# A second copy of the input, tokens along the partitions, for the first norm's sums of squares

## The chip, the cores and the metric

The kernel runs on one core of a Trainium2 chip, as one launch. The metric is the time of one execution on the device in microseconds (us). TensorE is called PE in the profile, VectorE DVE, ScalarE ACT, GpSimd POOL; SP is the engine whose queue issues the transfers here.

## The reference, cut to what matters

Two layers work on 256 tokens of 2048 features, in fp32. Layer 0 mixes by a long convolution beside a pool, layer 1 by a short convolution; each is followed by a gated feed-forward part (5632 wide), and a last norm ends it. Each part begins with an RMS norm; the first is that of the input x:

```python
def rms_norm(x, g):
    xf = x.astype(jnp.float32)
    y = xf * lax.rsqrt(jnp.mean(xf * xf, axis=-1, keepdims=True) + EPS)
    return (y * g.astype(jnp.float32)).astype(x.dtype)

def conv_pool_mixer(x, norm_g, w_in, conv_w, conv_b, ln_g, ln_b, w_pool, pool_scale, w_out):
    h = rms_norm(x, norm_g)
    u = h @ w_in
    a_val = u[..., :D_CONV]
    a_gate = u[..., D_CONV:2 * D_CONV]
    b_in = u[..., 2 * D_CONV:]
    a = a_val * jax.nn.sigmoid(a_gate)
    a = causal_depthwise_conv(a, conv_w) + conv_b
    a = jax.nn.silu(layer_norm(a, ln_g, ln_b))
    p = multiscale_pool(b_in, w_pool, pool_scale)
    return jnp.concatenate([a, p], axis=-1) @ w_out
```

## The kernel before, in words

Activations lie with features along the partitions: `h` holds 16 chunks of 128 features by 256 tokens. A product takes, for each chunk of outputs, one 128x128 block of weights for each of the 16 input chunks. Products must be as exact as fp32, so each weight and each activation is split into two fp32r halves, `hi` and `lo`, and a block costs three matmuls of 256 columns: hi times hi (L155), hi times lo (L156), lo times hi (L157). Later parts use a wide form with two matmuls (L152, L153).

The weights are one stream in the order of their use. `fetch` (L95 to L99) loads a unit of it on SP's queue, first 1, 3 and 4 blocks, then seven units of 8 blocks, then units of 16 blocks (1 MB). Four buffers hold the units, so a unit waits until the one four before it has been split. `prepare` (L101 to L111) makes the halves of a piece of 8 blocks: ACT casts it to `hi` (L109), DVE subtracts to get `lo` (L110). `next_block` (L113) does this four pieces ahead of the block that PE takes next. The framework orders each engine's instructions by a timeline of its own, with the written order as the priority: an instruction that is written later can be issued earlier, if what stands ahead of it still waits. Once built, each engine takes its instructions in that fixed order.

The start: x is loaded transposed, one or two chunks at a time (`load`, L320), between the first units of weights. For each chunk ACT and DVE multiply by the norm's gain and split into `xs` (`split`, L188 and L189). The factor 1/rms of each token is not needed for that: it is applied to the products' outputs. It comes from sums of squares: for each pair of chunks `square2` (L277) has ACT square 128x512 numbers (L280) and POOL add them to a running tile (L282). `rstd` (L287) calls `rsqrt_of` (L217): PE sums the running tile over the partitions by matmuls with a column of ones (L223), which leaves one number per token, tokens along the partitions, in two columns; ACT takes the square root (L225); DVE forms the reciprocal and corrects it (L226 to L231) and makes diagonal matrices of the factors (`diag`, L235); PE spreads them to all partitions (L243); DVE copies the result to `rstd` (L290).

The first product makes four chunks of outputs together (L411), so that each step over one input chunk takes four blocks; `loads_behind` (L327) issues the last loads of x and the rest of the vectors `v` behind the first steps. Then DVE scales the four outputs by `rstd` (L310), and the convolution begins: 31 taps a chunk, shared between POOL (with ACT's products, L364 and L366) and DVE (L375, L377), beside the further products of the mixer.

Of the kernel before, what the change touches and what calls it, by code (L numbers as in the profile page):

```python
# [11 lines left out]
F32 = mybir.dt.float32  # L12
F32R = mybir.dt.float32r
AF = mybir.ActivationFunctionType
ALU = mybir.AluOpType
PSUM = bass.MemoryType.PSUM

P = 128
T = 256
D = 2048  # L20
# [8 lines left out]
EPS = 1e-6  # L29
WINDOWS = (2, 4, 8, 16)  # L30

# the order of the first product's output after its first four chunks: chunks of the convolution,
# and groups of the pool
M0_ORDER = (
# [5 lines left out]

# columns of the per-feature vectors, one column per chunk of 128 features
VECS = {}
# [9 lines left out]

# blocks of 128x128 weights in the order of their use
N_BLOCKS = 24 * NC + 16 + NC * NC + 2 * (2 * NF * NC + NC * NF) + 48 * NC + NC * NC
# [10 lines left out]
UNIT_AT = [sum(UNITS[:u]) for u in range(len(UNITS))]  # L65
# units are split into halves in pieces: (unit, first block, blocks)
PIECE = 8
PIECES = [(u, o, min(PIECE, n - o)) for u, n in enumerate(UNITS) for o in range(0, n, PIECE)]
# pieces that are split, and units that are loaded, before they are needed
LOOK = 4  # L70
AHEAD = 1
# products that the tensor engine turns over before the first operands are there
WARM = 9
# taps of each pair of chunks of the long convolution that GpSimd adds up (VectorE takes the rest),
# and the pace of the work beside the matrix products in blocks a step
CONV = {1: (0, 2, 20), 3: (2, 2, 20), 5: (4, 2, 19), 6: (6, 1, 18), 7: (7, 1, 18)}
# [3 lines left out]
@with_exitstack  # L80
def block_kernel(ctx: ExitStack, tc: tile.TileContext, xT: bass.AP, vec: bass.AP, wall: bass.AP, out: bass.AP):
    nc = tc.nc
# [7 lines left out]

# [1 line left out]
    loaded, ready = {}, {}  # L92
    cursor = [0, 0]  # next block, piece of the next block

# [33 lines left out]

# [1 line left out]
    queues = {name: deque() for name in ("pool", "dve", "ln", "wait")}  # L130
# [28 lines left out]
    def matmul_chunks(xs, ks, n=1, wide=False, behind=None):  # L159
        """n chunks of 128 output features: hi*hi + hi*lo + lo*hi. When wide, columns 0:T hold  # L160
        hi*hi and T:2T the cross terms."""
        accs = [ps.tile([P, 2 * T], F32, name="acc") for _ in range(n)]
        for i, k in enumerate(ks):
            first, last = i == 0, i == len(ks) - 1
            for acc in accs:
                hi, lo = next_block()
                product(acc, hi, lo, xs[:, k, :], first, last, wide)
                tick()
            if behind is not None:
                behind(k)  # L170
        return accs

    phase = [None]  # the pool of the part of the kernel that is being built

# [7 lines left out]
    def split(dst, src, scale=None):  # L182
        """dst[:, :T], dst[:, T:] = fp32r halves of src (times a scale per feature)."""
        if scale is None:
            nc.scalar.copy(dst[:, :T], src)
            nc.vector.tensor_tensor(out=dst[:, T:], in0=src, in1=dst[:, :T], op=ALU.subtract)
        else:
            nc.scalar.activation(dst[:, :T], src, AF.Copy, scale=scale)  # L188
            nc.vector.scalar_tensor_tensor(out=dst[:, T:], in0=src, scalar=scale, in1=dst[:, :T], op0=ALU.mult, op1=ALU.subtract)  # L189

# [1 line left out]
    v = const.tile([P, NVEC], F32, name="v")  # L192
# [8 lines left out]
    nc.gpsimd.memset(ones, 1.0)  # L201
    # the tensor engine's clock rises after some microseconds of work
    idle = ps_st.tile([P, P], F32, name="idle", tag="st")
# [12 lines left out]

    def rsqrt_of(*totals, scale, halves=False):  # L217
        """(scale * sum over features and over totals + EPS) ** -0.5 per token, in every partition,
        if asked for in two halves. Tokens lie along the partitions in between."""
        st = ps_st.tile([P, 2], F32, name="st", tag="st")  # L220
        for i, x in enumerate(totals):
# [18 lines left out]
    def over_features(x):  # L240
        """Sum over the partitions, in every partition."""
        st = ps_st.tile([P, T], F32, name="st", tag="st")
        nc.tensor.matmul(st, ones, x, start=True, stop=True)  # L243
        return st

    class Norm:
        """RMS norm: h * gain goes into xs chunk by chunk; the factor per token follows."""

# [27 lines left out]

        def square2(self, c):  # L277
            """A pair of chunks."""
            into = tmp.tile([P, 2, T], F32, name="sum2" if c == 0 else "sq2", tag="sum2" if c == 0 else "gate", bufs=1 if c == 0 else 2)
            nc.scalar.activation(into, h[:, c : c + 2, :], AF.Square)  # L280
            if c:
                nc.gpsimd.tensor_tensor(out=self.pairs, in0=self.pairs, in1=into, op=ALU.add)  # L282
            else:
                self.pairs = into
                self.sums = [into[:, 0, :], into[:, 1, :]]

        def rstd(self):  # L287
            st = rsqrt_of(*self.sums, scale=1.0 / D)
            r = tmp.tile([P, T], F32, name="rstd", bufs=1)
            nc.vector.tensor_copy(out=r, in_=st)  # L290
            return r

    def project(src, ks, norm=None, wide=False, narrow_end=False):
        """h += src @ weights, and the next norm behind it."""
        for n in range(NC):
            if narrow_end and n == NC - 1:
                wide = False
            (acc,) = matmul_chunks(src, ks, wide=wide)
            if wide:
                t = phase[0].tile([P, T], F32, name="cross", bufs=3)  # L300
                nc.scalar.copy(t, acc[:, T:])
                nc.vector.tensor_tensor(out=h[:, n, :], in0=h[:, n, :], in1=t, op=ALU.add)
            nc.vector.tensor_tensor(out=h[:, n, :], in0=acc[:, :T], in1=h[:, n, :], op=ALU.add)
            if norm is not None:
                norm.add(n)
# [9 lines left out]

# [1 line left out]
    norm = Norm("mix_norm_e")  # L317
    nc.sync.dma_start(v[:, :NC], vec[:, :NC])

    def load(at, n):  # L320
        nc.sync.dma_start(h[:, at : at + n, :], xT[:, at : at + n, :])
        for c in range(at, at + n):
            norm.scale(c)
        if (at + n) % 2 == 0:
            norm.square2(at + n - 2)

    def loads_behind(k):  # L327
        if k < 3:
            load(10 + 2 * k, 2)
        if k == 2:  # L330
            nc.sync.dma_start(v[:, NC:], vec[:, NC:])

    load(0, 1)
    prepare(0)
# [11 lines left out]
    with tc.tile_pool(name="m0", bufs=1) as m0:  # L346
# [9 lines left out]
        def tap(c, n, k):  # L356
            """GpSimd's taps of n chunks."""
            dst = conv[:, c : c + n, :] if k == 0 else m0.tile([P, 2, T], F32, name="prod", bufs=4)[:, :n, :]
# [9 lines left out]
        def side_tap(c, n, k, first):  # L368
            """VectorE's taps, in a sum of their own."""
            if k == first:  # L370
# [18 lines left out]
        def convolve(c, n, taps):  # L389
            """The causal convolution of n chunks."""  # L390
            left = [2]
# [19 lines left out]
        first = matmul_chunks(xs, every, n=4, behind=loads_behind)  # L411
        r = norm.rstd()
        nc.scalar.activation(warm, r[:, :1], AF.Sigmoid)
# [4 lines left out]
        def pooled(g):  # L418
            """Windowed means minus the value, for a group of the pool."""
            w = WINDOWS[g]  # L420
# [29 lines left out]

        # layer norm over the features of the convolution, beside the pool's output projection
        state = {}
# [66 lines left out]

# [1 line left out]
    after = Norm("mix_norm_o")  # L521
    swiglu(norm, after)

# [1 line left out]
    norm = Norm("ffn_norm1")  # L525
    with tc.tile_pool(name="m1", bufs=1) as m1:
# [3 lines left out]
        r = None  # L530
# [20 lines left out]

# [1 line left out]
    last = Norm("final_norm", final=True)  # L553
# [17 lines left out]
def _blocks(w):  # L571
    """[K, N] -> [N/128, K/128, 128, 128]: output chunk, input chunk, input, output."""
    k, n = w.shape
    return w.reshape(k // P, P, n // P, P).transpose(2, 0, 1, 3)


def _cols(a):
    """[N] -> [128, N/128]"""
    return a.reshape(-1, P).T


def _layout(i):
# [49 lines left out]
    xT = i["x"][0].T.reshape(NC, P, T).transpose(1, 0, 2)  # L632
    return {"xT": np.ascontiguousarray(xT), "vec": np.ascontiguousarray(vec), "wall": wall}

# [14 lines left out]
```

## Time and profile before

| | before |
|---|---|
| time of three runs | 2149.3, 2149.49 (median), 2149.75 us |
| span of the profiled execution, first to last instruction | 2148.9 us |
| time of the profiled execution beyond its span | not listed; the median is 0.6 us above the span |
| PE busy | 2095.9 us, 98% |
| DVE busy | 1456.4 us, 68% |
| ACT busy | 1068.2 us, 50% |
| POOL busy | 202.2 us, 9% |
| mean granted clock of PE | 0.987 |
| transfers | 393.43 MB, mean 183 GB/s |

A row of the table by stretches gives, for one stretch, the busy time of each engine with the number of its instructions, the granted clock of PE (1.00 is 2.4 GHz, 0.50 is 1.2 GHz), the busy share of the 16 DMA engines and the rate. A row of the timeline is one instruction or several alike in a row; what stands in brackets is the engine's idle time before it and what ended it. The chain of waits follows the work that ended last back to the start: a row is a piece of time that the end depended on.

### The profile page before, as it was taken

What the parts mean: (1) busy time and instruction counts of PE and PEld (TensorE: products, weight loads), DVE (VectorE), ACT (ScalarE), POOL (GpSimd) and SP (SyncE); (2) the same over time, 40 slices, a digit from 0 to 9 for tenths busy, and PEclk for the clock granted to TensorE, in tenths of its full rate; (3) what the DMA queues carried; (4) which work ended last, traced back from release to release, by engine and by line L of the source; (5) the groups of instructions that cost most, each with busy time, mean ns of one, the idle gap of its engine ahead of it and who ended that gap; (6) DMA issues with size and microseconds to landing.
All of it is one profiled execution on the core that took longest, in us unless ns stands there. A gap on an engine that the chain in (4) does not pass through costs nothing.

```text
span 2148.9 us, 31546 instructions
## 1 busy us (share of the span) xinstructions
PE 2095.9 (98%) x12564; PEld 1869.5 (87%) x12564; DVE 1456.4 (68%) x1952; ACT 1068.2 (50%) x1595; POOL 202.2 (9%) x210
## 2 busy tenths in 40 slices
PE   8787999999999999999999999999999999999997
PEld 8787998888888888888888888888888888888887
DVE  7999886666555666666677777766666556666554
ACT  7655665444444444445444444554444444444553
POOL 3766420000000000001000000100000000000011
PEclk9889999999999999999999999999999999999999
DMA  7234455555555555555455555555555555555551
GB/s 280 83 134 157 160 200 190 187 186 196 187 186 195 183 190 196 185 188 194 179 196 184 189 197 184 188 184 189 196 187 187 195 180 193 196 184 189 196 180 75
DMA packets 56851, 393.43 MB, mean 183 GB/s; under 512 B 6400, under 2 KB 7424, under 8 KB 9984
## 3 DMA queue, kind: packets, MB, share of 16 engines
q1 hardware_dynamic: 56704, 391.42, 51.1%
q8 instruction: 98, 1.61, 0.3%
q14 instruction: 49, 0.40, 0.1%
HBM read 389.30 MB, written 2.10 MB: 182 GB/s over the span
## 4 chain that ended last, share of the span: by engine, by line
PE 89%; DVE 8%; issue 1%; ACT 1%; DMA 0%; SPq 0%; DVEq 0%
PE acc L152 56%; PE acc L153 29%; DVE side L377 3%; DVE lo L110 2%; PE acc L157 1%; PE acc L156 1%; PE acc L155 1%; DVE sw L430 0%; ACT xs L188 0%; ACT hi L109 0%; DMA h<-in_xT 0%; DVE a_in L407 0%; DVE h L559 0%; DVE side L375 0%; DVE conv L381 0%
## 5 line engine op out<-in xcount | busy, mean ns | idle before, releaser
L110 DVE TENSOR_TENSOR lo<-w,hi 128x1024 fp32r<-128x1024 f32 (+1 forms) x740 | 921.9, 1247 | 632.5 <-ACT hi L109 628.7
L109 ACT CAST hi<-w 128x1024 fp32r<-128x1024 f32 (+1 forms) x740 | 775.7, 1050 | 949.1 <-PE acc L152 622.4
L152 PE MATMUL acc<-xs,hi 128*128 128x512 f32 x3584 | 1243.3, 391 | 0.0
L153 PE MATMUL acc<-xs,lo 128*128 128x256 f32 x3584 | 1003.9, 280 | 0.0
L152 PEld LDWEIGHTS acc<-xs,hi 128*128 128x128 f32 x3584 | 670.3, 187 | 146.9
L153 PEld LDWEIGHTS acc<-xs,lo 128*128 128x128 f32 x3584 | 677.3, 189 | 0.1
L152 PE MATMUL acc<-y,hi 128*128 128x512 f32 x1386 | 485.2, 393 | 0.0
L153 PE MATMUL acc<-y,lo 128*128 128x256 f32 x1386 | 386.1, 279 | 0.0
L152 PEld LDWEIGHTS acc<-y,hi 128*128 128x128 f32 x1386 | 259.4, 187 | 62.1
L153 PEld LDWEIGHTS acc<-y,lo 128*128 128x128 f32 x1386 | 259.7, 187 | 0.4
L273 POOL TENSOR_TENSOR sumsq<-sumsq,sq 128x256 f32<-128x256 f32 x56 | 57.5, 1026 | 1587.8 <-ACT sq L271 1587.8
L157 PE MATMUL acc<-xs,lo 128*128 128x256 f32 x512 | 150.3, 302 | 31.4 <-DVE lo L110 31.2
L155 PE MATMUL acc<-xs,hi 128*128 128x256 f32 x512 | 151.3, 299 | 3.3 <-ACT hi L109 3.3
L156 PE MATMUL acc<-xs,hi 128*128 128x256 f32 x512 | 150.6, 297 | 0.0
L157 PEld LDWEIGHTS acc<-xs,lo 128*128 128x128 f32 x512 | 103.7, 206 | 34.5 <-DVE lo L110 34.3
L366 POOL TENSOR_TENSOR conv<-conv,prod 128x512 f32<-128x512 f32 (+1 forms) x90 | 124.0, 1379 | 62.8 <-ACT prod L364 56.9
L155 PEld LDWEIGHTS acc<-xs,hi 128*128 128x128 f32 x512 | 105.8, 207 | 3.8 <-ACT hi L109 3.7
L156 PEld LDWEIGHTS acc<-xs,hi 128*128 128x128 f32 x512 | 105.7, 207 | 0.1
L152 PE MATMUL acc<-z,hi 128*128 128x512 f32 x256 | 89.6, 393 | 0.0
L177 ACT COPY cross<-acc 128x256 f32<-128x256 f32 x224 | 81.7, 365 | 0.0
L377 DVE SCALAR_TENSOR_TENSOR side<-a_in,v,side 128x256 f32<-128x256 f32 x86 | 77.3, 919 | 0.4
L153 PE MATMUL acc<-z,lo 128*128 128x256 f32 x256 | 71.3, 279 | 0.0
(116 smaller groups left out, 1172.9 us busy)
## 6 DMA issues: line engine op xcount, KB each, us to landing
w<-in_wall SPq DMA_DIRECT2D x365, 1024.0 KB, 4.8
w<-in_wall SPq DMA_DIRECT2D x7, 512.0 KB, 7.1
h<-in_xT SPq DMA_DIRECT2D x7, 256.0 KB, 7.2
out<-h SPq DMA_DIRECT2D x3, 512.0 KB, 2.7
v<-in_vec SPq DMA_DIRECT2D x1, 260.0 KB, 6.6
h<-in_xT SPq DMA_DIRECT2D x2, 128.0 KB, 2.6
w<-in_wall SPq DMA_DIRECT2D x1, 256.0 KB, 3.9
out<-h SPq DMA_DIRECT2D x2, 128.0 KB, 1.9
```

The source lines that it names most:

```text
L109: nc.scalar.copy(hi[:, : n * P], w)
L110: nc.vector.tensor_tensor(out=lo[:, : n * P], in0=w, in1=hi[:, : n * P], op=ALU.subtract)
L152: nc.tensor.matmul(acc, hi, x, start=first, stop=False, skip_group_check=True)
L153: nc.tensor.matmul(acc[:, T:], lo, x[:, :T], start=False, stop=last, skip_group_check=True)
L155: nc.tensor.matmul(acc[:, :T], hi, x[:, :T], start=first, stop=False)
L156: nc.tensor.matmul(acc[:, :T], hi, x[:, T:], start=False, stop=False)
L157: nc.tensor.matmul(acc[:, :T], lo, x[:, :T], start=False, stop=last)
L177: nc.scalar.copy(t, acc[:, T:])
L273: nc.gpsimd.tensor_tensor(out=self.sums[0], in0=self.sums[0], in1=sq, op=ALU.add)
L366: nc.gpsimd.tensor_tensor(out=conv[:, c : c + n, :], in0=conv[:, c : c + n, :], in1=dst, op=ALU.add)
L377: nc.vector.scalar_tensor_tensor(out=dst, in0=src, scalar=wt, in1=dst, op0=ALU.mult, op1=ALU.add)
```

## The change

x is also handed over as `xtok`: 128 partitions, each with two tokens' rows of 2048 features, 8 KB a row. Behind the steps 4 and 8 of the first product one row for each partition is loaded (1 MB on SP's queue) into a single buffer `rows`, and ACT squares it in place, 128x2048, with the sum along the row going to a column of `rowsq`. The calls of `square2` are gone, and with them POOL's adds; `rsqrt_of` is handed `rowsq` in the place of the tile that PE's column sums wrote, and no totals, so that L223 issues nothing for this norm. The buffer's pool is opened ahead of the mixer and closed before the feed-forward part. The diff without its comments and docstrings:

```diff
-def block_kernel(ctx: ExitStack, tc: tile.TileContext, xT: bass.AP, vec: bass.AP, wall: bass.AP, out: bass.AP):
+def block_kernel(ctx: ExitStack, tc: tile.TileContext, xT: bass.AP, xtok: bass.AP, vec: bass.AP, wall: bass.AP, out: bass.AP):
...
-    def rsqrt_of(*totals, scale, halves=False):
-        st = ps_st.tile([P, 2], F32, name="st", tag="st")
+    def rsqrt_of(*totals, scale, halves=False, st=None):
+        if st is None:
+            st = ps_st.tile([P, 2], F32, name="st", tag="st")
...
-        def square2(self, c):
-            into = tmp.tile([P, 2, T], F32, name="sum2" if c == 0 else "sq2", tag="sum2" if c == 0 else "gate", bufs=1 if c == 0 else 2)
-            nc.scalar.activation(into, h[:, c : c + 2, :], AF.Square)
-            if c:
-                nc.gpsimd.tensor_tensor(out=self.pairs, in0=self.pairs, in1=into, op=ALU.add)
-            else:
-                self.pairs = into
-                self.sums = [into[:, 0, :], into[:, 1, :]]
-
-        def rstd(self):
-            st = rsqrt_of(*self.sums, scale=1.0 / D)
+        def rstd(self, sums=None):
+            st = rsqrt_of(*self.sums, scale=1.0 / D, st=sums)
...
-        if (at + n) % 2 == 0:
-            norm.square2(at + n - 2)
...
         if k == 2:
             nc.sync.dma_start(v[:, NC:], vec[:, NC:])
+        if k in (4, 8):
+            j = (k - 4) // 4
+            rows = x0_pool.tile([P, D], F32, name="rows")
+            nc.sync.dma_start(rows, xtok[:, j, :])
+            nc.scalar.activation(rows, rows, AF.Square, accum_out=rowsq[:, j : j + 1])
+
+    x0 = ctx.enter_context(ExitStack())
+    x0_pool = x0.enter_context(tc.tile_pool(name="x0", bufs=1))
+    rowsq = const.tile([P, 2], F32, name="rowsq")
...
-        r = norm.rstd()
+        r = norm.rstd(rowsq)
...
+    x0.close()
...
+    xtok = i["x"][0].reshape(2, P, D).transpose(1, 0, 2)
```

## Rows read from the trace of the kernel before

**Rows 1.** The page: its first line, and PE's busy time and share.
```profile
span 2148.9 us, 31546 instructions
...
PE 2095.9 (98%) x12564; PEld 1869.5 (87%) x12564; DVE 1456.4 (68%) x1952; ACT 1068.2 (50%) x1595; POOL 202.2 (9%) x210
```
**Rows 2.** The table by stretches: stretch, length, busy times, PE's clock, DMA share, rate.
```profile
9.40:11.90 2.50, 0.00 (x0) 0.00 (x0) 0.88 (x2) 2.38 (x5) 0.87 (x1) 1.00 1.03 408
11.90:15.70 3.80, 3.77 (x18) 3.60 (x19) 3.79 (x4) 3.80 (x8) 2.02 (x3) 0.58 1.03 404
...
23.60:25.50 1.90, 0.01 (x1) 0.00 (x0) 1.90 (x2) 1.89 (x2) 0.83 (x1) 1.00 0.00 0
25.50:30.00 4.50, 4.44 (x24) 4.44 (x25) 4.50 (x9) 0.00 (x0) 0.00 (x0) 0.62 0.66 233
30.00:38.60 8.60, 8.60 (x75) 8.60 (x74) 7.18 (x13) 4.93 (x6) 0.00 (x0) 1.00 0.98 386
38.60:50.60 12.00, 12.00 (x101) 11.95 (x100) 9.94 (x19) 10.06 (x19) 1.49 (x2) 1.00 0.83 312
50.60:220.00 169.40, 134.17 (x974) 131.16 (x974) 168.98 (x183) 102.40 (x196) 112.21 (x82) 0.89 0.34 121
...
240.00:2149.00 1909.00, 1897.98 (x11119) 1675.83 (x11117) 1229.11 (x1686) 918.69 (x1325) 66.07 (x75) 1.00 0.52 186
```
**Rows 3.** The chain of waits, 0 to 62 us: start, length, what.
```profile
23.22 2.30 DVE lo L110
25.56 0.75 PE acc L157 x4
...
30.19 0.79 PE st L223 x8
...
38.75 0.43 PE st L243 x2
```
**Rows 4.** The table by stretches for L155 alone (one matmul a block).
```profile
0.00:15.70 15.70, 4.75 (x14) 0.90 0.81 277
15.70:38.60 22.90, 14.46 (x50) 0.92 0.77 288
```
**Rows 5.** The table by stretches for DVE: first L110, then L189.
```profile
11.90:25.40 13.50, 7.18 (x4) 0.87 0.74 279
...
11.90:25.40 13.50, 6.77 (x6) 0.87 0.74 279
```
**Rows 6.** DVE's timeline, 25 to 34 us.
```profile
25.43 2.45 DVE L189 SCALAR_TENSOR_TENSOR xs<-h,v,xs 128x256 fp32r<-128x256 f32 x6
27.81 3.48 DVE L110 TENSOR_TENSOR lo<-w,hi 128x1024 fp32r<-128x1024 f32 x3
...
32.68 2.35 DVE L110 TENSOR_TENSOR lo<-w,hi 128x1024 fp32r<-128x1024 f32 x2
```
**Rows 7.** Lines L280 and L282: ns min/median/max, first and last start.
```profile
L280 ACT ACTIVATE sq<-h x7: 612/615/619, 10.3 to 22.0; 128x512 f32<-128x512 f32 x7
...
L282 POOL TENSOR_TENSOR sum<-sum,sq x7: 1267/1412/1871, 11.0 to 23.1; 128x512 f32<-128x512 f32 x7
```
**Rows 8.** ACT's timeline, 10 to 34 us.
```profile
10.86 1.03 ACT L109 CAST hi<-w 128x1024 fp32r<-128x1024 f32 x1
...
31.01 0.26 ACT L225 ACTIVATE inv<-st,eps 128x2 f32<-128x2 f32 x1 [5.52 <-PE st L223]
```
**Rows 9.** SP's timeline from 12 us: the rest of `v`, then weights from unit 7.
```profile
12.79 0.33 SPq L331 DMA_DIRECT2D v<-in_vec  x1
13.49 47.66 SPq L99 DMA_DIRECT2D w<-in_wall  x12
```
**Rows 10.** Transfers issued at 12.8, 13.5 and 25.5 us: size, us to landing.
```profile
v<-in_vec SPq DMA_DIRECT2D x1, 260.0 KB, 6.6
...
w<-in_wall SPq DMA_DIRECT2D x1, 512.0 KB, 7.1
...
w<-in_wall SPq DMA_DIRECT2D x1, 1024.0 KB, 4.7
```

More of the change, by code (lines that the diff above doesn't have):

```diff
@@ L632, in _layout @@
     xT = i["x"][0].T.reshape(NC, P, T).transpose(1, 0, 2)
-    return {"xT": np.ascontiguousarray(xT), "vec": np.ascontiguousarray(vec), "wall": wall}
+    xtok = i["x"][0].reshape(2, P, D).transpose(1, 0, 2)
+    return {"xT": np.ascontiguousarray(xT), "xtok": np.ascontiguousarray(xtok), "vec": np.ascontiguousarray(vec), "wall": wall}
 def kernel(**inputs):
```

## The prediction, made before the changed kernel ran

> **What bounds the kernel now.** I read the page first: TensorE (PE) is busy for 98% of a span of 2148.9 us [rows 1], so only the stretches in which PE loses time matter. The table by stretches finds them. From 240 us to the end PE is busy for 1898 of 1909 us at the full granted clock [rows 2]; nothing of the change runs there, so whatever is won or lost before 240 us reaches the end unchanged. From 50.6 to 220 us VectorE (DVE) is busy for 169.0 of 169.4 us while PE is busy for 134 [rows 2]: this is the convolution, bound by DVE. Before it lies the start, in which the change sits.
>
> In the start the first product (64 blocks of weights, three matmuls a block) is late. PE stands still from 9.4 to 11.9 us and from 23.6 to 25.5 us, and behind each of these the granted clock falls to a mean of 0.58 and 0.62, mostly the lower of its two levels, 1.2 GHz [rows 2]. The chain of waits names what ended the second one: DVE's `lo` split (L110), then the lo products (L157), then the eight records of the norm's own column sums (L223, 0.79 us), up to the product that spreads the factor (L243), which stands behind the whole first product in PE's order [rows 3]. In all this time DVE has no gap before 30 us [rows 2], and it is slow: while GpSimd (POOL) adds the squares, four `lo` splits and six `xs` scalings take 7.18 and 6.77 us [rows 5]; with POOL quiet, three splits take 3.48 us (1.16 each) and six scalings 2.45 us (0.41 each) [rows 6]. The same ten instructions would take 4 x 1.16 + 6 x 0.41 = 7.1 us alone, so 13.95 - 7.1 = 6.85 us is lost beside seven POOL adds of about 1.4 us [rows 7].
>
> **What the change removes.** (a) POOL's seven adds: POOL itself waits for nothing else here, so their worth is DVE's 6.85 us. (b) The eight Squares of 128x512 on ScalarE (ACT), 0.62 us each, 4.9 us by their durations [rows 7]. (c) PE's column sums, 0.79 us on the chain [rows 3].
>
> How much of (a) and (c) reaches the end? Not 6.85: PE is the next limit. At 15.7 us PE has run 14 of its 64 blocks; the other 50 take until 38.6 us, 22.9 us [rows 4]. At 0.12 us a matmul (101 in 12.0 us at full clock [rows 2]) they need 50 x 3 x 0.12 = 18.0 us, so that the product could end at 33.7 us. The difference is **4.9 us**: 1.9 of standing still, about 1.6 of half clock (24 matmuls in 4.44 us instead of 2.9), 0.8 of L223 [rows 2, 3], and 0.6 of short waits. All of these come from the late `lo` or from L223. The first stop, 9.4 to 11.9 us, I leave in: it ends when the first pairs of x and the fourth unit of weights have landed and been cast, and the transfers are at a share of 1.03 then [rows 2].
>
> **What it adds.** Two Squares of 128x2048 with a sum along the row. The nearest rows are 0.615 us for 512 and 1.03 us for 1024 columns [rows 7, 8], so 0.42 us per 512: 1.87 us. Taking out the sum has no row; I bound it by nothing and by a small activation, 0.26 us [rows 8]. Two make 3.7 to 4.3 us, against the 4.9 removed: ACT's sum is about even, but the work moves to later, into the 5.5 us that ACT now waits for L223 [rows 8]. Covered by that wait it costs nothing; without it, up to 2 us in front of a cast.
>
> Two transfers of 1 MB on SP's queue. SP's order is not the written one: the rest of `v`, written behind units 7 and 8 of the weights (counted from 0), is issued at 12.8 us, ahead of unit 7 at 13.5, because that one waits for its buffer [rows 9]. So I expect the first row load right behind `v`, about 13.1 us. The `v` load landed 6.6 us after its issue, at 19.4 [rows 9, 10]; at some 400 GB/s, the rate of the full stretches [rows 2], 1 MB takes 2.6 us more: landed at 22.0, squared at 23.9. Unit 7, issued at 13.5, landed at 20.6 [rows 9, 10], and moves to 23.2; cast (1.03) and split (1.16) it is ready at 25.4. PE wants it after 40 of its 64 blocks, at 15.7 + 26 x 0.36 = 25.1, the lo half some 1 us later: just in time.
>
> The second row load has the same single buffer, so it waits for the first Square, and weight loads behind it in SP's order wait too. Issued at 24, it lands at 28.7 with an empty queue (1 MB in 4.7 us [rows 10]), or 2.6 later for each 1 MB of weights ahead of it: 28.7, 31.3 or 33.9. Square (1.87) and the chain from the Sqrt at 31.01 to the `lo` splits at 32.68 that follow the `diag` tile in DVE's order, 1.7 us [rows 6, 8], make the factor's operand ready 3.6 us later: 32.3, 34.9 or 37.5. L243 wants it at 33.7. I take the two nearer cases, a wait of 0 to 1.2, and put down **0.5 us**; the far end, 3.8, stays for the range.
>
> First what the rows show: in the full stretch 512 KB took 7.1 us to land, in a quiet one 1 MB took 4.7 [rows 10], so a transfer issued there stands in a backlog. The Trainium skill ("DMA: Bandwidth & Descriptors", section "Queues, rings and completion order") says that each DMA engine consumes one queue's descriptors in ring order; by it the second load of x delays every later unit of weights by its whole time, which speaks against this change. By the rows alone the delay of a unit is 0 to 2.6 us per row load; I used 2.6.
>
> What is late next: with the start shortened, DVE has less time for the splits ahead of the second product. Up to two of them (2.3 us) can slide behind the factor; DVE now has 1.4 and 2.1 us of idle time in 30 to 50.6 us [rows 2], which takes them, so I count nothing, at worst 2.3. The 8 KB for the rows are given back before the feed-forward part, at a place where it waits for the mixer's buffers anyway: nothing.
>
> **Sum.** 4.9 - 0.5 = 4.4 us. The span of the profiled execution is 2148.9 us; the page lists no other time for it, and the median of the three runs, 2149.49, is 0.6 above, which I carry over unchanged: **2145.1 us**. That is 0.2% (4.3 us), about what a measurement of this kernel can tell from no change: the forecast lies on that line.
>
> **The rivals.**
> (1) More than the forecast. DVE is without a gap from 11.9 to 30 us and again in the convolution [rows 2], so if DVE alone sets the end, all 6.85 us of (a) come back: 2142.6. Against it: the factor cannot come before PE's 33.7 us, and DVE would be idle before that. Chance 0.15.
> (2) Weights late behind the rows. If PE waits 1 to 2 us for the unit of the eleventh step, and the clock falls once more (1.6 us, as above), 3 us of the 4.4 go: 2148.1. For it: the margin of 0 to 1 us above, and the order in the queue. Against it: a quiet stretch follows, with a transfer share of 0.00 at 23.6 to 25.5 us [rows 2]. Chance 0.18.
> (3) Slower: PE's order places the factor's product too early. L223 now stands amid the first product, after some 45 blocks [rows 3, 4]. Were L243 put there, PE would reach it at 15.7 + 31 x 0.36 = 26.9 us and stand until 32.3, 34.9 or 37.5: 5.4 to 10.6 us, plus 1.6 of half clock, less the 4.9 won: +2.1, +4.7, +7.3. The middle gives **2154.2**. It decides against the change once the wait is over 3.3 us. For it: PE takes its queue in order, and the operand now comes by two transfers one behind the other. Against it: L243 stands at the product's end now though its operand was ready 6 us before. Chance 0.13.
> (4) The removal is real but the convolution gives it back through another order of DVE's and POOL's work there; 2149.5. Nothing in the rows speaks for it beyond 112 us of POOL work beside DVE [rows 2]. Chance 0.04.
>
> **How the numbers follow.** The forecast's case has 0.50, with an own range of 2143.5 to 2146.5, and lies half on either side of the line: 0.27 faster, 0.23 same. Faster by over 0.2%: 0.27 + 0.15 = 0.42. Same: 0.23 + 0.18 + 0.04 and 0.04 of the third rival = 0.49. Slower: the rest of the third, 0.09. The range reaches from the first rival's 2142.6, a little widened, to the second and fourth with the lower end of the third: 2142.0 to 2151.5.
>
> **What would show it.** Right: `lo` splits of 1.1 to 1.2 us and `xs` of 0.41 us from 12 us on; no stop of PE at 23 us and a clock of 1.00 from 16 us; L243 at 34 us instead of 38.6; the convolution's DVE stretch starting and ending 4 to 5 us earlier. Wrong: ACT idle before a Square for the row transfer with casts behind it, PE standing before L243 or before an L155 whose weights have not landed, or an end of the DVE-bound stretch that has not moved with L243.

## The result, and the profile after

The changed kernel takes **2155.94 us** (median of seven runs, 2155.27 to 2157.81), the kernel before 2149.75 us in the runs beside it: a ratio of **1.0031 [1.0021, 1.0042]**. It is slower, by 0.3%, and the forecast of 2145.1 us and its range up to 2151.5 us both miss it. The profiled execution has a span of 2153.4 us, 4.5 above that of before, and a time of 2155.27 us, so 1.9 us lie beyond the span. In later runs of the kernel before, beside the first experiments, the median time is 2149.43 us and the median span 2147.5 us: there too 1.9 us lie beyond the span, and the execution of before that was profiled, with its 2148.9 us, was 1.4 us longer than usual. So the two profiles place only 4.5 us of the 6.2 us between the medians.

The first part of the change did what it was said to do. The table by stretches of the kernel after (columns as in [rows 2]):

```profile
11.90:15.70 3.80, 3.45 (x17) 3.45 (x18) 3.47 (x5) 3.60 (x7) 0.00 (x0) 0.58 1.03 402
...
23.60:25.50 1.90, 1.90 (x19) 1.90 (x18) 0.30 (x1) 1.90 (x4) 0.00 (x0) 1.00 1.03 423
25.50:30.00 4.50, 4.50 (x38) 4.30 (x37) 3.50 (x4) 3.05 (x4) 0.00 (x0) 1.00 1.01 397
...
258.00:264.00 6.00, 0.10 (x2) 0.01 (x1) 3.39 (x7) 5.96 (x10) 0.00 (x0) 0.81 0.40 138
264.00:270.00 6.00, 6.00 (x33) 6.00 (x34) 2.56 (x4) 2.48 (x5) 0.00 (x0) 0.62 0.25 105
```

The stop of PE at 23.6 us and the half clock behind it are gone: 1.00 where [rows 2] had 0.62. The same view for L155 alone, against [rows 4]:

```profile
0.00:15.70 15.70, 4.79 (x14) 0.90 0.81 275
15.70:33.50 17.80, 13.04 (x49) 0.99 1.02 409
```

Fourteen blocks have begun by 15.7 us, as before, and 63 of the 64 by 33.5 us. PE's timeline has the end of the 64th and the first matmul behind it:

```profile
34.13 0.28 PE L157 MATMUL acc<-xs,lo 128*128 128x256 f32 x1
34.26 0.28 PE L155 MATMUL acc<-xs,hi 128*128 128x256 f32 x1
```

So the first product gives way at 34.26 us; in the kernel before it did so at 38.59, when L243 started. That is 4.3 us earlier. DVE's groups from 11.9 to 25.4 us (count, then busy time in us and mean ns of one, then the idle time before them), which answer to [rows 5]:

```profile
L110 DVE TENSOR_TENSOR lo<-w,hi 128x1024 fp32r<-128x1024 f32 x5 | 6.1, 1225 | 4.4 <-ACT hi L109 4.3
L189 DVE SCALAR_TENSOR_TENSOR xs<-h,v,xs 128x256 fp32r<-128x256 f32 x12 | 5.1, 478 | 0.0
```

A split takes 1.23 us instead of 1.80 (7.18/4), a scaling 0.48 instead of 1.13 (6.77/6). Yet the factor is later than before. DVE's timeline of the kernel before (start, length, and in brackets the idle time before):

```profile
39.22 0.42 DVE L290 COPY rstd<-st 128x256 f32<-128x256 f32 x1 [1.92 <-PE st L243]
...
43.28 0.75 DVE L407 TENSOR_TENSOR a_in<-val,gate 128x256 f32<-128x256 f32 x2
...
235.80 0.41 DVE L458 TENSOR_TENSOR total<-total 128x256 f32<-128x256 f32 x1
...
261.30 0.69 DVE L485 TENSOR_TENSOR cat<-conv,cat 128x512 fp32r<-128x512 f32 x1 [2.30 <-ACT cat L484]
```

The same of the kernel after; its lines 245, 282, 405, 456 and 483 are 243, 290, 407, 458 and 485 of before:

```profile
34.28 0.61 DVE L237 TENSOR_SCALAR diag<-v,inv,err 128x128 f32<-128x128 f32 x2
...
40.04 0.43 DVE L282 COPY rstd<-st 128x256 f32<-128x256 f32 x1 [2.89 <-PE st L245]
40.38 1.22 DVE L110 TENSOR_TENSOR lo<-w,hi 128x1024 fp32r<-128x1024 f32 x1
...
42.84 3.49 DVE L110 TENSOR_TENSOR lo<-w,hi 128x1024 fp32r<-128x1024 f32 x3
46.24 0.76 DVE L405 TENSOR_TENSOR a_in<-val,gate 128x256 f32<-128x256 f32 x2
...
238.50 0.42 DVE L456 TENSOR_TENSOR total<-total 128x256 f32<-128x256 f32 x1
...
263.97 0.69 DVE L483 TENSOR_TENSOR cat<-conv,cat 128x512 fp32r<-128x512 f32 x1 [2.61 <-ACT cat L482]
```

What to see, in order. `diag`, the operand of the spread product, is ready at 34.89 us (34.28 + 0.61). DVE then waits 2.89 us for PE's L245, and copies the factor at 40.04, 0.8 us later than before. Four splits stand between the factor's copy and the first convolution input `a_in` (1.22 and 3.49 us); before, two did. So `a_in` starts 3.0 us later (46.24 against 43.28), the convolution's last sum 2.7 later (238.50 against 235.80), and the first `cat` of the layer norm 2.7 later (263.97 against 261.30). PE's timeline tells why the factor is late:

```profile
39.30 0.28 PE L155 MATMUL acc<-xs,hi 128*128 128x256 f32 x1
39.41 0.59 PE L245 MATMUL st<-diag,ones 128*128 128x256 f32 x2
39.66 0.47 PE L156 MATMUL acc<-xs,hi 128*128 128x256 f32 x1
```

PE is not waiting: it has weights for the products behind the first one, and L245 stands amid them. The trace has 79 records of L155 ahead of it; before, 64 stood ahead of L243, the whole first product and nothing else. At the end of the mixer the head start that PE won is paid back. PE's waits from 215 to 300 us, first of before, then of after (total us, times, longest):

```profile
PE acc L155 <- ACT cat L484: 0.2, 1, 0.2
```

```profile
PE acc L155 <- ACT cat L482: 5.9, 1, 5.9
```

PE stands 5.9 us for the layer norm's output, and the granted clock is 0.62 in the six microseconds behind it. From the first `cat` to the end of the span it takes 1889.4 us (2153.4 - 264.0) instead of 1887.6: 1.8 more. A clock that is 38% lower for six microseconds would be enough for that (2.3 us), but this is worked out and not shown by a run. So the span's +4.5 is 2.7 by the later `cat` and 1.8 behind it.

### The profile page after: what moved, and what is told of

Same layout as the page of the kernel before. It is cut to its first block, busy times and chain, and to the rows that moved or that the text cites. A ratio compares the mean times of both kernels' runs of the same rounds, so it can differ in the third digit from the quotient of the medians.

```text
span 2153.4 us, 31525 instructions
## 1 busy us (share of the span) xinstructions
PE 2093.0 (97%) x12556; PEld 1867.6 (87%) x12556; DVE 1452.1 (67%) x1952; ACT 1069.3 (50%) x1591; POOL 196.2 (9%) x203
## 4 chain that ended last, share of the span: by engine, by line
PE 91%; DVE 7%; issue 1%; ACT 0%; DMA 0%; SPq 0%; DVEq 0%
PE acc L152 56%; PE acc L153 29%; DVE side L375 3%; PE acc L155 2%; DVE lo L110 2%; PE acc L157 2%; PE acc L156 2%; DVE sw L428 0%; DMA w<-in_wall 0%; DVE side L373 0%; DVE h L559 0%; DVE a_in L405 0%; PE st L225 0%; DVE cat L435 0%; ACT conv L480 0%
## 5 line engine op out<-in xcount | busy, mean ns | idle before, releaser
L110 DVE TENSOR_TENSOR lo<-w,hi 128x1024 fp32r<-128x1024 f32 (+1 forms) x740 | 919.8, 1244 | 638.9 <-ACT hi L109 635.0
L155 PE MATMUL acc<-xs,hi 128*128 128x256 f32 x512 | 149.3, 294 | 3.6 <-ACT hi L109 3.6
L155 PEld LDWEIGHTS acc<-xs,hi 128*128 128x128 f32 x512 | 104.2, 204 | 4.1 <-ACT hi L109 4.1
```

Of the source, the lines that this page charges most:

```text
L110: nc.vector.tensor_tensor(out=lo[:, : n * P], in0=w, in1=hi[:, : n * P], op=ALU.subtract)
L155: nc.tensor.matmul(acc[:, :T], hi, x[:, :T], start=first, stop=False)
```

## The experiments

Three theories were held against each other. **A:** the end follows the start of the convolution's work on DVE, which is about equally long in every build, and that start follows the place of the spread product in PE's order. **B:** the 2 MB more of transfers make weights late. **C:** the order of the work inside the convolution has changed. For the kernel after itself the table below answers C: its convolution takes 191.5 us, in the kernel before 191.8. Eight kernels ran. The table gives what they came to; all times in us, from the timelines as above. "Factor" is the start of the copy to `rstd`, "inputs" the end of the second of the first two `a_in`, "conv" from there to the last sum of the convolution, "norm" from that sum to the first `cat`, "rest" from it to the end of the span, "stop" PE's wait for `cat`.

| kernel | median | ratio to before, 95% | factor | inputs | conv | norm | rest | stop |
|---|---|---|---|---|---|---|---|---|
| before | 2149.4 to 2149.8 | 1 | 39.22 | 44.03 | 191.8 | 25.5 | 1887.6 | 0.2 |
| after | 2155.94 | 1.0031 [1.0021, 1.0042] | 40.04 | 47.00 | 191.5 | 25.5 | 1889.4 | 5.9 |
| spread_first | 2147.64 | 0.9992 [0.9983, 1.0000] | 35.93 | 41.75 | 190.5 | 25.7 | 1888.0 | 0 |
| small_adds | 2145.28 | 0.9980 [0.9971, 0.9989] | 34.60 | 39.42 | 192.1 | 25.5 | 1887.8 | 0.2 |
| spread_late | 2156.81 | 1.0032 [1.0019, 1.0045] | 43.41 | 49.19 | 187.8 | 28.0 | 1890.1 | 3.5 |
| two_buffers | 2149.61 | 1.0000 [0.9991, 1.0009] | 35.66 | 42.63 | 191.8 | 25.4 | 1887.9 | 0.2 |
| loads_only | 2155.78 | 1.0026 [1.0016, 1.0036] | 37.55 | 43.27 | 192.9 | 27.8 | 1890.5 | 3.5 |
| units_first | 2152.44 | 1.0014 [1.0005, 1.0023] | 35.47 | 43.14 | 191.2 | 27.3 | 1889.4 | 3.5 |
| dve_adds | 2145.52 | 0.9980 [0.9971, 0.9988] | 36.04 | 41.21 | 189.3 | 25.8 | 1887.4 | 0.2 |
| dve_adds_74 | 2147.00 | 0.9989 [0.9980, 0.9998] | 37.02 | 42.20 | 188.7 | 25.5 | 1887.9 | 0.2 |

**The spread product back behind block 64.** The kernel after, with one dependency more: the mixer's products that had come in front of the factor's product are held behind it.

```diff
-        nc.tensor.matmul(st, ones, x, start=True, stop=True)
+        spread_by.append(nc.tensor.matmul(st, ones, x, start=True, stop=True).ins)
...
         r = norm.rstd(rowsq)
+        factor = spread_by[-1]
...
-            (acc_v,) = matmul_chunks(xs, every)
-            (acc_g,) = matmul_chunks(xs, every)
+            with tc.issue_after(factor) if i == 2 else ExitStack():
+                (acc_v,) = matmul_chunks(xs, every)
+                (acc_g,) = matmul_chunks(xs, every)
```

> The changed kernel with one edge in PE's order: the product that spreads the factor (L245 in the changed kernel, behind 78 blocks) stands directly behind the 64 blocks of the first product, as it did before the change. Theory A (DVE's convolution stretch has a fixed length of about 192 us and starts when the factor is there): the factor is copied at about 35.5 us instead of 40.0, the first a_in comes at 40.5 to 42 instead of 46.2, and the time falls by 4 to 6 us from 2155.9, to 2150 to 2152. Theory B (the loss comes from the 2 MB of row transfers that slow the weights): nothing moves, 2155 to 2157. Theory C (the loss comes from another order and another overlap of DVE and POOL inside the convolution): the time does not follow the a_in, it may end anywhere between 2149 and 2158.

Measured: 2147.64 us, 8.3 below the kernel after. Its PE timeline, then DVE's:

```profile
35.03 0.67 PE L247 MATMUL st<-diag,ones 128*128 128x256 f32 x2 [0.60 <-DVE diag L237]
```

```profile
35.93 0.42 DVE L284 COPY rstd<-st 128x256 f32<-128x256 f32 x1
...
41.00 0.75 DVE L407 TENSOR_TENSOR a_in<-val,gate 128x256 f32<-128x256 f32 x2
...
232.26 0.41 DVE L460 TENSOR_TENSOR total<-total 128x256 f32<-128x256 f32 x1
...
257.98 0.69 DVE L487 TENSOR_TENSOR cat<-conv,cat 128x512 fp32r<-128x512 f32 x1 [2.29 <-ACT cat L486]
```

PE now waits 0.60 us for the operand, and the factor comes 4.1 us earlier than in the kernel after, `a_in` 5.2, the convolution's last sum 6.2, the `cat` 6.0; PE's stop there is gone, and the rest is 1.4 shorter. A is right in direction; the gain is larger than the move of the factor: three splits instead of four stand between the factor and `a_in`, PE's stop goes, and the convolution takes 1.0 us less, for which no run shows a reason. The transfers are the same in both kernels, so B is not what makes the kernel after slower than before. The two profiles also differ in the clock from 11.9 to 15.7 us (1.00 here, 0.58 there), but that is not the gain: here PE stands 1.8 us at 23.4 us for a cast, and the last matmul of the first product starts at 34.15 us, in the kernel after at 34.13.

**The contention alone.** The kernel before, with POOL's adds cut to eight columns of each chunk, so that only a small part of the sums of squares is gathered.

```diff
-                nc.gpsimd.tensor_tensor(out=self.pairs, in0=self.pairs, in1=into, op=ALU.add)
+                nc.gpsimd.tensor_tensor(out=self.pairs[:, :, :8], in0=self.pairs[:, :, :8], in1=into[:, :, :8], op=ALU.add)
```

> The kernel before, with POOL's seven adds cut to 8 of each 256 columns, so that the sums of squares are incomplete; all orders near the factor stay as they were, with the spread behind block 64. It prices the contention alone. If the prediction's step was right (DVE loses 6.85 us beside the adds, of which PE can take 4.1 to 4.9): the first product ends at about 34 instead of 38.6 us, the first a_in comes some 4 to 5 us earlier than 43.3, and the time is 2145 to 2146.5. If the contention is worth nothing at the end: 2149 to 2150. Theory A gives the first, since here the factor moves with the product; B and C say nothing of it.

Measured: 2145.28 us, 4.2 below before. DVE's timeline:

```profile
34.60 0.42 DVE L290 COPY rstd<-st 128x256 f32<-128x256 f32 x1 [1.07 <-PE st L243]
...
38.66 0.76 DVE L407 TENSOR_TENSOR a_in<-val,gate 128x256 f32<-128x256 f32 x2
...
231.55 0.41 DVE L458 TENSOR_TENSOR total<-total 128x256 f32<-128x256 f32 x1
```

With the adds small and nothing else changed, the spread product starts at 33.97 us in PE's timeline; the factor, `a_in` and the convolution's last sum come 4.6, 4.6 and 4.3 us earlier than before. This kernel keeps L223, so the prediction's figure for it is 4.9 less 0.8, 4.1 us: the contention was priced rightly.

**The factor late in the kernel before.** One chunk of the products that come later is taken ahead of the factor's product.

```diff
+        (ahead,) = matmul_chunks(xs, every)
         r = norm.rstd()
...
-            (acc_v,) = matmul_chunks(xs, every)
+            (acc_v,) = [ahead] if i == 2 else matmul_chunks(xs, every)
```

> The kernel before, with the norm's factor asked for one chunk (16 blocks) later in the written order, so that the spread stands behind 80 blocks instead of 64. No row transfer, POOL's adds unchanged. Theory A: the factor comes 5.8 us later (45 us), the first a_in at 47 to 49 us instead of 43.3, since one or two weight splits are done in the meantime; the time rises by 3.5 to 6 us, to 2153 to 2156. Theory B: no transfer is added, 2149 to 2150. Theory C: no figure.

Measured: 2156.81 us, 7.4 above before, with nothing of the change in it: a kernel without the change, but with a late spread product, is as slow as the kernel after. DVE's timeline:

```profile
43.41 0.42 DVE L290 COPY rstd<-st 128x256 f32<-128x256 f32 x1 [0.64 <-PE st L243]
...
48.43 0.76 DVE L407 TENSOR_TENSOR a_in<-val,gate 128x256 f32<-128x256 f32 x2
...
236.99 0.41 DVE L459 TENSOR_TENSOR total<-total 128x256 f32<-128x256 f32 x1
```

The time is 0.8 us above A's range, and its parts are not A's. `a_in` is 5.2 us later, but the last sum only 1.2: the convolution took 187.8 us instead of 191.8. The norm took 2.5 more, and the rest 2.5 more with PE's stop of 3.5 us. So "equally long" holds to some 2 us only, and PE's head start has a price of its own.

**The second row load in a buffer of its own.** The kernel after, with the second row loaded into `conv`, which is not yet in use, so that the two rows have a buffer each.

```diff
-            rows = x0_pool.tile([P, D], F32, name="rows")
+            rows = conv.rearrange("p a t -> p (a t)") if j else x0_pool.tile([P, D], F32, name="rows")
```

> The changed kernel, with the second row load going into the convolution's buffer, which is not in use yet, so that it doesn't wait for the first Square. Both loads are then issued at about 14 to 16 us, the second ahead of units 8 and 9 of the weights; the spread stands behind block 64. Theory A: the factor is copied at 34.5 to 36 us, the first a_in comes at 40.5 to 42.5, 2150 to 2152, although the weights are disturbed more and earlier. Theory B: more transfers in the tight stretch, PE waits for units 8 and 9, no gain: 2155 to 2158. Theory C: no figure.

Measured: 2149.61 us, level with before and 6.3 below the kernel after. DVE's timeline:

```profile
35.66 0.42 DVE L282 COPY rstd<-st 128x256 f32<-128x256 f32 x1 [1.02 <-PE st L245]
...
38.47 3.49 DVE L110 TENSOR_TENSOR lo<-w,hi 128x1024 fp32r<-128x1024 f32 x3
41.87 0.76 DVE L405 TENSOR_TENSOR a_in<-val,gate 128x256 f32<-128x256 f32 x2
```

With the second row earlier, L245 stands behind 64 blocks again, with no dependency put in: the factor comes at 35.66 us. PE now waits 1.8 us for casts between 12 and 60 us (in the kernel after, none from 15 to 60), and the splits stay in front of `a_in` (6.2 us from factor to `a_in`, as after; before 4.06). What A gives is mostly won, and the splits take their part.

**The transfers alone.** small_adds with the two row loads, nobody reading them, and the spread product held behind the first product.

```diff
+        if k in (4, 8):
+            nc.sync.dma_start(conv.rearrange("p a t -> p (a t)"), xtok[:, (k - 4) // 4, :])
...
-        nc.tensor.matmul(st, ones, x, start=True, stop=True)
+        with tc.issue_after(newest[0]) if not spread_by else ExitStack():
+            spread_by.append(nc.tensor.matmul(st, ones, x, start=True, stop=True))
```

> small_adds (sums of squares incomplete, from 8 of each 256 columns) with the two row transfers of the changed kernel added, at the same places in SP's order, the second waiting for the first; nobody reads the rows. The spread stays behind block 64. It prices the transfers alone. Theory A: the transfers are hidden, the factor comes at 34.5 to 35.5 us and the first a_in at 37.5 to 40, as in small_adds; 2144.5 to 2147. Theory B (the transfers slow the weights): PE waits for weights before 50 us, 2148 or more.

Measured: 2155.78 us, 10.5 above small_adds: a miss for A. ACT's timeline, then PE's, then DVE's:

```profile
24.71 0.26 ACT L226 ACTIVATE inv<-st,eps 128x2 f32<-128x2 f32 x1 [2.17 <-PE st L224]
24.87 2.93 ACT L109 CAST hi<-w 128x1024 fp32r<-128x1024 f32 x3
```

```profile
25.96 0.39 PE L155 MATMUL acc<-xs,hi 128*128 128x256 f32 x1 [1.28 <-ACT hi L109]
...
36.92 0.59 PE L245 MATMUL st<-diag,ones 128*128 128x256 f32 x2
```

```profile
39.35 0.41 DVE L411 TENSOR_TENSOR a_in<-val,gate 128x256 f32<-128x256 f32 x1
...
42.86 0.41 DVE L411 TENSOR_TENSOR a_in<-val,gate 128x256 f32<-128x256 f32 x1
```

ACT waits for the column sums with three casts behind the square root in its order; PE stands 1.28 us for the first of them, and the clock halves (0.63 from 27 to 30 us), so L245 runs at 36.92 us, not at 34. The two `a_in` come 3.5 us apart, with splits between them, and at the layer norm PE stands 3.5 us. So something costs time here, by the order of ACT's and DVE's work: the loads, or the hold on the spread product that came in with them, which this run doesn't tell apart. In the kernel after itself PE waits for no weight from 15 to 60 us, so this is not how it lost its time; B is out for that kernel, and not shown wrong in general.

**Weights ahead of the rows.** two_buffers with the dependency of spread_first, and each row load held behind a unit of weights.

```diff
+            with tc.issue_after(sent[7 + j]):
+                nc.sync.dma_start(rows, xtok[:, j, :])
```

> The changed kernel with the second row load going into the convolution's buffer, the row loads put behind unit 7 and unit 8 of the weights in SP's order, and the spread directly behind block 64. Theory A: no wait of PE for weights, the factor at 34.5 to 35.5 us, the first a_in at 38.5 to 40 (two weight splits stand ahead of it), 2145 to 2148, below both kernels. Theory B: as two_buffers, 2149 to 2151.

Measured: 2152.44 us; 2145 to 2148 was expected. DVE's timeline:

```profile
39.53 0.42 DVE L408 TENSOR_TENSOR a_in<-val,gate 128x256 f32<-128x256 f32 x1
39.86 2.35 DVE L110 TENSOR_TENSOR lo<-w,hi 128x1024 fp32r<-128x1024 f32 x2
42.73 0.41 DVE L408 TENSOR_TENSOR a_in<-val,gate 128x256 f32<-128x256 f32 x1
```

The factor came at 35.47 us, as expected, the second `a_in` behind two splits 3.2 us after the first, and the norm took 27.3 us with a stop of PE of 3.5. An early factor alone does not win; what DVE puts behind it, and the layer norm, count too.

**Without POOL and without loads.** The kernel before with its adds on DVE, whole in what it computes: once with the dependency of spread_first (dve_adds) and once without (dve_adds_74).

```diff
-                nc.gpsimd.tensor_tensor(out=self.pairs, in0=self.pairs, in1=into, op=ALU.add)
+                nc.vector.tensor_tensor(out=self.pairs, in0=self.pairs, in1=into, op=ALU.add)
```

> The kernel before, with the seven adds of squares on DVE instead of POOL, whole, and the spread directly behind block 64. No row transfer. DVE pays 7 x 0.68 us (a 128x512 add of two SBUF operands without POOL, as the convolution's L381 takes) = 4.8 us for the 6.85 us it lost beside POOL, and it pays in a stretch where it would otherwise stand idle. Theory A: the first product ends at 34 to 35 us, the factor comes at 34.8 to 36, the first a_in at 39 to 41, 2145.5 to 2148.5. Theory C (what POOL does at the start is of no account): 2149 to 2150.

> dve_adds without the edge in PE's order: the spread then stands behind 74 blocks instead of 64, nothing else is asked to change. Theory A: 10 blocks of 0.36 us put the factor 3.6 us later (39 to 40 us) and the first a_in at 43 to 45; the time rises by 3 to 5 us over dve_adds' 2145.5, to 2148.5 to 2150.5. If the place of the spread were of no account: 2145 to 2146.5. Theory C (orders inside the convolution decide by themselves): no figure, it may also fall.

Measured: 2145.52 us and 2147.00 us, both below both kernels. PE's timeline of the first, then of the second:

```profile
34.74 0.67 PE L245 MATMUL st<-diag,ones 128*128 128x256 f32 x2
```

```profile
36.39 0.59 PE L243 MATMUL st<-diag,ones 128*128 128x256 f32 x2
```

Without the dependency, 74 blocks stand ahead of the spread product, with it 64. The difference is 1.5 us of time where 3 to 5 were expected. In the two profiles the spread products ran 1.65 us apart and not ten blocks' 3.6 (10 x 0.36), because the 64 blocks ended 1.8 us earlier in dve_adds_74: PE's first stop ended there at 10.69 us, in dve_adds at 12.07, and the clock behind it differs. First dve_adds, then dve_adds_74:

```profile
11.90:15.70 3.80, 3.63 (x19) 3.63 (x20) 3.65 (x5) 3.80 (x9) 0.00 (x0) 0.60 1.03 405
```

```profile
11.90:15.70 3.80, 3.76 (x32) 3.75 (x32) 3.80 (x7) 3.80 (x8) 0.00 (x0) 1.00 1.03 401
```

PE ran 19 matmuls in the one and 32 in the other. The direction is A's, but the intervals of the two ratios overlap, and each of these profiles is one execution: the size stays open.

## Why the prediction was wrong

**Right, by its own steps.** The gain of (a): 4.2 us in small_adds, against 4.1, the 4.9 less L223's 0.8. PE's first product ends at 34.3 us (33.7 was forecast), with no stop at 23 us and no half clock behind it: 4.3 of the 4.9 us came. The first row load was issued at 13.79 us and landed 8.4 later, at 22.2 (22.0 was forecast), unit 7 at 15.11 + 8.4 = 23.5 (23.2); PE waited for neither in the kernel after. The landings of the first row load and of unit 7 in the kernel after, against [rows 10], by issue at 13.79 and 15.11 us:

```profile
rows<-in_xtok SPq DMA_DIRECT2D x1, 1024.0 KB, 8.4
w<-in_wall SPq DMA_DIRECT2D x1, 512.0 KB, 8.4
```

Unit 7, issued 1.3 us behind the row load, landed 1.3 us behind it, 2.9 us later than before. The Trainium skill's ring order ("DMA: Bandwidth & Descriptors", "Queues, rings and completion order") and this trace agree. ACT's timeline after, where each Square waits for its transfer, the first with three casts behind it:

```profile
22.22 1.91 ACT L326 ACTIVATE rows<-rows 128x2048 f32<-128x2048 f32 x1 [1.64 <-DMA rows<-in_xtok]
24.04 0.19 ACT L326 ACTIVATION_READ_ACCUMULATOR rows<-rows 128x1 f32 x1
...
31.06 1.91 ACT L326 ACTIVATE rows<-rows 128x2048 f32<-128x2048 f32 x1 [0.45 <-DMA rows<-in_xtok]
```

A Square takes 1.91 us (1.87 was forecast) and its sum 0.19 (0 to 0.26). The operand of the spread product was ready at 34.89, the middle of the three values named, 34.9.

That PE did not wait for unit 7 is luck, as far as the profiles tell. Its cast stood behind the first Square, whose transfer ACT waited for (1.64 us idle, the sign that the prediction gave for being wrong), and ended at 25.17 us; PE came to that unit's first block at 25.36. In spread_first and two_buffers PE was there sooner and stood 1.8 and 1.5 us. This is the second rival's wait; the clock did not fall behind it (1.00 from 25.5 to 30 us in both).

**The step that failed** is "L243 wants it at 33.7", and the 0.5 us put down on it. It took for granted that PE takes the spread product right behind the first product, as in [rows 3], and would wait there for its operand. The built order has it 15 blocks further back (79 L155 ahead, not 64). So an operand that came 0.6 us behind the first product's end (34.89 against 34.26) became a spread product 5.7 us later than the 33.7 of the forecast (39.41), and no wait of PE shows it, since PE does other work in between. The runs show this term on both sides: with the product back behind block 64 the kernel after wins 8.3 us (spread_first), and with the product 16 blocks later the kernel before loses 7.4 (spread_late); in both, other parts moved with it. The third rival named this instruction's place as the danger, but on the wrong side: too early, with PE standing. Why the order came out so is an inference: it is laid down when the kernel is built, by a timeline in which a later operand lets other products pass. Two kernels without the dependency fit that: two_buffers, whose operand is ready at 32.4 us, ahead of the first product's end (64 blocks), and dve_adds_74, whose operand is ready at 33.5 us, behind it (74 blocks). No run shows the timeline itself.

**The term counted as nothing.** Splits that slide behind the factor were bounded by 2.3 us and put at 0, as DVE's idle time would take them. Four instead of two stand between the factor and `a_in` in the kernel after: 6.2 us instead of 4.06, so **2.1 us**, nearly the whole bound.

**The term that was missing.** What is won before 240 us "reaches the end unchanged" was the ground of the sum. PE kept its own head start (the first product ended 4.3 us earlier) while DVE's chain moved later, so PE ran into the layer norm and stood for 5.9 us, where it had stood for 0.2. Behind the stop, with the granted clock at 0.62, another **1.8 us** went. The table bears this out, though not in proportion: the rest takes 1887.4 to 1888.0 us in every kernel with a stop of 0.2 us or none, and 1889.4 to 1890.5 in the four with a stop of 3.5 us or more.

**The sum again.** The forecast had the factor 4.4 us earlier, it came 0.8 later: 5.2. Of these, 4.1 are PE's order (40.04 against 35.93 with the product back in its place); the other 1.1 are missing in spread_first too, where the spread product starts at 35.03 us instead of the forecast's 34.2 and a split stands ahead of the copy. With 2.1 for the splits and 1.8 behind PE's stop, less 0.3 that the convolution and the norm were shorter, this is 8.8 over the forecast's span (2145.1 - 0.6 = 2144.5), so 2153.3; the profile has 2153.4. The time beyond the span was carried over as 0.6 and is 1.9 in the kernel after: another 1.3 us of the miss. But it is 1.9 in the kernel before as well. The 0.6 set the span of one long execution against the median of others, so these 1.3 us are no cost of the change beyond its span; they lie somewhere within it, where the two profiles don't show them.

**What stays open.** The norm stretch takes 25.4 to 25.8 us in some builds and 27.3 to 28.0 in others (spread_late, loads_only, units_first, the three with a stop of 3.5 us). The traces tell where: in these three, ACT's cast and its load of the square root's table (1.28 us) end only as the square root starts, 2.2 to 3.0 us behind the start of the last sum of squares (L473 of before); in the others ACT has them done, waits 0.5 to 0.8 us for PE's sums, and starts 1.1 to 1.5 us behind it. In these three, DVE also has a split between the copy of the norm's factor and the scaling with it. Why the builds order them so is not shown. A version of the kernel after in which PE's stop at the layer norm alone is taken away was not tried, so the 1.8 us rest on what the table shows together. Nor is it known why the convolution takes 187.8 us in one build and 192.9 in another.

## What to carry to other kernels

When a change makes an operand later, ask not only how long its reader would wait but what the build will put in front of that reader instead: a product passed over shows no wait at all, and cost more here (4.1 us of the factor) than the wait would have (0.60 us in spread_first). Follow the one instruction that starts the bound stretch (here the factor's copy and the first `a_in`) through both traces before any totals. And where contention is the cost, moving the work off the contending engine can be cheaper than rebuilding it: seven adds moved from POOL to DVE, with the spread product held at its place, give 2145.52 us against 2149.56 of before in the same runs, 0.9980 [0.9971, 0.9988].

## What was not expected of the hardware

- Behind PE's last stop before 12.3 us, the granted clock from 11.9 to 15.7 us was 0.58 (before), 0.58 (after), 0.60 (dve_adds), 1.00 (spread_first) and 1.00 (dve_adds_74). The stop was not equally long: 2.54, 2.78 and 2.20 us in the first three, 1.67 and 0.72 in the last two. Stops of about one length came out both ways: 2.15 us in small_adds with a clock of 0.63, 2.25 us in loads_only with 1.00. Thirteen matmuls more in that stretch (32 against 19), at 0.12 us each, are about 1.6 us of PE's work.
- ACT's sum along the row is an instruction of its own behind the Square, 0.19 us for 128x1, beside 1.91 us for the 128x2048 squares.
